# A planner's clock, its rule for early weights and its resting tiles, in an ordered two-block transformer kernel

## The chip, the cores and the metric

The kernel runs on one core of a Trainium2 chip. TensorE does the matrix products, ScalarE and VectorE the elementwise work, GpSimd a few small operations; transfers from device memory are issued from SyncE's queue. The metric is device time in microseconds (us) of one execution; lower is better.

## The reference

One sequence of 256 tokens, width 1024, float32 throughout, passes three layers. The first layer is a mixer (gated causal convolution and forgetting attention, one input projection) and a gated feed-forward of hidden width 2816. The second and third have attention (eight heads, a position bias; the third takes a difference of two softmaxes) and the same feed-forward, and each norm of them is modulated by a vector `c`:

```python
mod = (c_act @ ada_w[i] + ada_b[i])[:, None, :]
sh_a, sc_a, g_a, sh_f, sc_f, g_f = jnp.split(mod, 6, axis=-1)
h = rms_norm(x, norm_g[i, 0]) * (1.0 + sc_a) + sh_a
y = attention(h, ...)
x = x + g_a * rms_norm(y, norm_g[i, 1])
h = rms_norm(x, norm_g[i, 2]) * (1.0 + sc_f) + sh_f
x = x + g_f * rms_norm(swiglu_2(h, ffn_w_in[i], ffn_w_out[i]), norm_g[i, 3])
```

All weights are read once, some 227 MB in all, 50 MB of them `ada_w`.

## The kernel before

**Products.** Every large product is made of three products of fp32r operands. A weight tile of 128x512 float32 (called `raw` where the transfer puts it) is split into `hi` (ScalarE, a copy) and `lo` (VectorE, raw minus hi); activations are split the same way (`hTh`/`hTl`, `pair`). Three matmuls x_hi·w_hi, x_hi·w_lo, x_lo·w_hi add up in a bank of the matmul accumulator. The 256 tokens are two halves `h` of 128 rows. Split weights live in 16 pairs of slots (`hi`, `lo`), and in the feed-forwards in 8 more (`wp`). Transfers of `raw` go through three buffers of 1 MB.

**The order.** The program is one long order written by a planner that runs while the kernel is built. Class `Order` has a clock `now` that only TensorE's instructions and its idle time move: `mm` (a matmul) and `tr` (a transposition) add their planned time to it. Each other engine is a `Lane` with the time at which it comes free (`A` ScalarE, `V` VectorE, `G` GpSimd, `S` SyncE) and a cost for each operation. Tasks are generators that yield the time at which they go on; after each matmul `pump` runs the tasks whose time has come and then `fill`. So where an instruction stands in its engine's program depends on the planned times alone; on the chip every engine runs its own program strictly in that order and waits for what isn't ready. `pin` fixes the order.

**Weights.** `fill` issues the transfer of the next `raw` when a buffer is free by the plan, puts the next `hi` on ScalarE when the transfer has come by the plan (`come`) and ScalarE is free, and then `lo` on VectorE. `dma` plans a transfer at 360 bytes per ns after all transfers planned earlier, and 1.1 us more.

**Chains of norms.** `chain(h, ...)` is what stands between two big products: squares of the result (ScalarE), the root (`rstd`, GpSimd), the new `x` (VectorE, two instructions), its squares, the second root, the normalized tile `ch` (VectorE one half, ScalarE the other), eight transpositions on TensorE, modulation and splits. While half 0 is in its chain TensorE works on half 1's product. A chain raises `o.urgent`, and `fill` then takes weights only where an engine is free at once (slack 0 unless fewer than `ENOUGH` units are in stock). There are ten chains that end in transpositions and two, at the end, that end in the output.

**Modulation.** `ada` computes `c_act @ ada_w` on VectorE: 96 pieces of 512 KB go through two buffers `araw`, each with two multiply-adds into `asum`. Its pace follows the plan: piece i not before `t0 + i * ADA_EARLY`, never in a chain, and not while weights are short unless `t0 + i * ADA_LATE` has passed. Then `araws.give(t, r)` hands the buffer back at planned time r, and the next piece's transfer may be issued. All transfers of weights and of `ada_w` stand in one queue, SyncE's, in planned order; an issue that waits for its buffer holds back those behind it.

Of the kernel before, what the change touches and what calls it, by code (L numbers as in the profile page):

```python
# [13 lines left out]
F32R = mybir.dt.float32r  # L14
# [17 lines left out]
SLACK = 0.5  # L32
ENOUGH = 4
STOCK = 9
ADA_START, ADA_EARLY, ADA_LATE = 30.0, 5.5, 8.0
HEADS_1, HEADS_2 = 9.0, 2.0
PAD_END = 104
LAG = 3


# [67 lines left out]
class Order:  # L108
# [29 lines left out]
    def mm(self, out, lhsT, rhs, start, stop, shared=False):  # L138

        self.pin(self.pe, self.nc.tensor.matmul(out, lhsT, rhs, start=start, stop=stop, skip_group_check=shared))  # L140
        n = math.prod(out.shape[1:])
        self.now += n / 2400 * (1 if rhs.dtype == F32R else 4)
        return self.now + 0.2

    def tr(self, out, src, ident):
        self.pin(self.pe, self.nc.tensor.transpose(out, src, ident))  # L146
        self.now += 0.107
        return self.now + 0.2

    def spawn(self, gen, at=0.0):  # L150
# [62 lines left out]
def block_kernel(ctx: ExitStack, tc: tile.TileContext, a: dict, onehot: bass.AP, out: bass.AP):  # L213
    nc = tc.nc
    o = Order(tc)
# [7 lines left out]
    def ring(pool, name, n, shape, dtype=F32):  # L223
        return Ring([pool.tile(shape, dtype, name=f"{name}{i}") for i in range(n)])

    def small(name, shape, dtype=F32):
        return cst.tile(shape, dtype, name=name)
# [3 lines left out]
    araws = ring(cst, "araw", 2, [P, 1024])  # L231
# [32 lines left out]
    def ffn_stream(w_gu, w_dn, where):  # L264
# [3 lines left out]
        def up(s):  # L268
            for k0 in (0, 4):
                stream.append(Raw(gu[:, k0:k0 + 4, :, s * 256:(s + 1) * 256], 4, 512, where))  # L270

        def down(s):
            stream.append(Raw(dn[:, 2 * s:2 * s + 2, :], 2, 1024, where))
# [3 lines left out]
        for s in range(2, STEPS - 1):  # L277
            up(s)
            if s - 1 < STEPS - LAG:
                down(s - 1)  # L280
        up(STEPS - 1)
        for s in range(STEPS - LAG, STEPS):
            down(s)
# [21 lines left out]
    def issue_raw():  # L305
        r = stream[pos["raw"]]
        pos["raw"] += 1
        r.tile = raws.take()
        if len(r.ap.shape) == 4:
            dst = r.tile.rearrange("p (k g c) -> p k g c", g=2, c=r.w // 2)  # L310
            for g in range(2):
                r.arrival = o.dma(dst[:, :, g], r.ap[:, :, g])
        else:
            r.arrival = o.dma(r.tile[:, :r.nk * r.w].rearrange("p (k c) -> p k c", c=r.w), r.ap)

    def fill(force=False):

        slack = SLACK if not o.urgent or pos["lo"] - pos["first"] < ENOUGH else 0.0
        while True:
            while pos["raw"] < len(stream) and raws.when() is not None and raws.when() <= o.now:  # L320
                issue_raw()
            some = False
            if pos["unit"] < len(units) and pos["unit"] - pos["lo"] < 3:
                u = units[pos["unit"]]
                pool = more if u.where and more.when() is not None and more.when() <= o.now else slots
                come = u.raw.arrival is not None and u.raw.arrival <= o.now
                place = pool.when() is not None and pool.when() <= o.now
                if come and place and (force or A.free <= o.now + slack):
                    some = True
                    pos["unit"] += 1  # L330
                    u.pool, u.slot = pool, pool.take()
                    u.hi, u.lo = (t[:, :u.w] for t in u.slot)
                    u.hi_ready = A.activation(u.hi, u.raw.tile[:, u.at:u.at + u.w], AF.Copy)
            if pos["lo"] < pos["unit"]:
                u = units[pos["lo"]]
                if force or max(V.free, u.hi_ready) <= o.now + slack:
                    some = True
                    pos["lo"] += 1
                    u.ready = V.tensor_sub(u.lo, u.raw.tile[:, u.at:u.at + u.w], u.hi.bitcast(F32), after=u.hi_ready)
                    u.raw.left -= 1  # L340
                    if not u.raw.left:
                        raws.give(u.raw.tile, u.ready)
            force = False
            if not some:
                return
# [5 lines left out]
    def take(n):  # L351
        got = [u for r in stream[pos["use"]:pos["use"] + n] for u in r.units]
        pos["use"] += n
        return got
# [27 lines left out]
    def product(ps, pair, h, ks, us, marks=None, first=True, last=True):  # L382

        n = len(us)
        for i, (k, u) in enumerate(zip(ks, us)):
            if marks is not None:
                o.wait(marks[h][k // 4])
            c = slice(h * P, (h + 1) * P)
            t = triple(ps, pair[0][:, k, c], pair[1][:, k, c], u, first and i == 0, last and i == n - 1)
        return t  # L390
# [190 lines left out]
    def load_gain(src, gain):  # L581
        gain.tile = yield from o.get(gains)
        gain.load.t = o.dma(gain.tile, src.to_broadcast([P, D]))
# [46 lines left out]
    def ada():  # L630
        yield from o.until(c_mark)
        pieces = [(l, what, cc, k0) for l, what in ada_order for cc in range(2) for k0 in range(0, 8, 2)]
        loaded, t0 = [], o.now
        for i in range(len(pieces) + 1):
            if i < len(pieces):
                l, what, cc, k0 = pieces[i]
                c0 = parts_of.index(what) * D + cc * 512
                if k0 == 0:
                    if what[0] == "g" and cc == 0:
                        o.spawn(load_gain(a["norm_g_2"][l, 1 if what == "g_a" else 3].unsqueeze(0), gated[l, what]))  # L640
                    sums = yield from o.get(asum)
                    r = G.memset(sums, 0.0)
                    yield r
                    ba = o.dma(sums[0:1, :], a["ada_b_2"][l:l + 1, c0:c0 + 512])
                t = yield from o.get(araws)
                arrival = o.dma(t.rearrange("p (k c) -> p k c", c=512),
                                a["ada_w_2"][l].rearrange("(k p) c -> p k c", p=P)[:, k0:k0 + 2, c0:c0 + 512])
                loaded.append((l, what, cc, k0, t, max(arrival, ba), sums))
            if i:
                l, what, cc, k0, t, arrival, s = loaded.pop(0)  # L650
                yield max(arrival, t0 + i * ADA_EARLY)
                while (o.urgent or V.free > o.now + SLACK or
                       pos["lo"] - pos["first"] < STOCK and o.now < t0 + i * ADA_LATE):
                    yield o.now + 0.2
                for k in range(2):
                    r = V.scalar_tensor_tensor(s, t[:, k * 512:(k + 1) * 512], c_act[:, k0 + k:k0 + k + 1], s,
                                               op0=OP.mult, op1=OP.add)
                    yield r - 0.3
                araws.give(t, r)
                if k0 == 6:  # L660
                    o.spawn(ada_finish(l, what, cc, s, r), r)


    def scope(**kinds):

        stack, got = ExitStack(), {}
        for name, (n, shape, dtype) in kinds.items():
            got[name] = ring(stack.enter_context(tc.tile_pool(name=name, bufs=1, reuse_waits="tile")), name, n, shape, dtype)
        return stack, got
# [87 lines left out]

    small("pad_end", [P, PAD_END])
    phase, sc = scope(qp=(4, [P, 4, 256], F32), gp=(8, [P, 512], F32),
# [195 lines left out]
    for k0 in (0, 4):  # L955
        for h in range(2):
            t = product(fb[h][:, :260], hT, h, range(k0, k0 + 4), us_f[k0:k0 + 4], hm, k0 == 0, k0 == 4)
# [50 lines left out]
    for n in range(2):  # L1008
        us = take(1)
        o.wait(ya_mark)  # L1010
        for h in range(2):
            ps = o.hold(banks)
            t = product(ps, yaT, h, range(4), us)
# [22 lines left out]
    for h in range(2):  # L1036
        for n in range(2):
            ps = o.hold(banks)
            t = product(ps, ybT, h, range(4), ub[n])
# [23 lines left out]
    def ffn(hm, gb, **kw):  # L1063
# [25 lines left out]
        def up(s, h):  # L1089
            if s not in us_of:  # L1090
                us_of[s] = take(2)
            act_mark[s, h] = Mark()
            ps = o.hold(banks)
            t = product(ps, hT, h, allk, us_of[s], hm)
            o.spawn(activate(s, h, ps), t)
# [14 lines left out]
        def downs(s):  # L1110
            for h in range(2):
                for n in range(2):
                    down(s, h, n)
# [6 lines left out]
        for s in range(2, STEPS - 1):  # L1120
            up(s, 0)
            up(s, 1)
            if s - 1 < STEPS - LAG:
                downs(s - 1)
        us_of[STEPS - 1] = take(2)
        for s in range(STEPS - LAG, STEPS):
            dn[s] = take(1)
        for h in range(2):
            up(STEPS - 1, h)
            o.spawn(chain(h, ys[h], gb, out_marks, **kw))  # L1130
            for s in range(STEPS - LAG, STEPS):
                for n in range(2):
# [237 lines left out]
```

## Time and profile before

| | us |
|---|---|
| median of 3 runs | 990.28 (989.15 to 990.47) |
| the profiled execution, its own time | 993.5 |
| its span, first to last instruction | 991.6 |
| TensorE busy | 975.9 |
| VectorE busy | 739.2 |
| ScalarE busy | 605.2 |
| mean granted TensorE clock | 0.997 of full |

The rows come from the one profiled execution, whose time is 3.2 us above the median. A busy TensorE isn't proof of a full one: matmuls overlap in the records, so the rate is read from the starts of a run of them. In a timeline row the number in brackets is the idle time of the engine before the row and what ended it.

### The profile page before, as it was taken

How to read it: one execution, taken by the hardware profiler on the slowest of the kernel's cores; microseconds unless marked ns; L12 is line 12 of the kernel's file. 1: busy time of each engine (PE TensorE's matmuls, PEld its weight loads, DVE VectorE, ACT ScalarE, POOL GpSimd, SP SyncE). 2: the span in 40 equal slices, each digit the busy share in tenths (PEclk: the TensorE clock that was granted, in tenths of full speed). 3: DMA queues.
4: the chain of work that ended last, by engine and by line, in shares of the span. 5: the costliest groups of instructions: out<-in, count | busy, mean ns of one | idle time of the engine just before them, and what ended most of it. 6: DMA issues, size and time to landing. Idle time of an engine off the chain costs nothing.

```text
span 991.6 us, 14032 instructions
## 1 busy us (share of the span) xinstructions
PE 975.9 (98%) x4814; PEld 808.5 (82%) x4814; DVE 739.2 (75%) x1469; ACT 605.2 (61%) x1286; POOL 35.2 (4%) x65
## 2 busy tenths in 40 slices
PE   7999999999999999999999999999999999999997
PEld 6888778888888888898788888888897888888886
DVE  5897879889888958887799888747765786464632
ACT  6746666774555537866685454637788795464531
POOL 1000000000000001000000000001000100000000
PEclk9999999999999999999999999999999999999999
DMA  6969778679989875775759989645542567646401
GB/s 217 361 202 308 254 263 271 218 231 319 363 287 326 294 257 189 253 258 173 233 187 313 369 274 314 231 138 194 176 163 86 172 206 253 211 157 207 163 33 43
DMA packets 143539, 227.19 MB, mean 229 GB/s; under 512 B 5991, under 2 KB 78932, under 8 KB 143468
## 3 DMA queue, kind: packets, MB, share of 16 engines
q1 hardware_dynamic: 143452, 226.30, 68.0%
q8 instruction: 37, 0.61, 0.2%
q14 instruction: 34, 0.28, 0.1%
q10 hardware_dynamic: 16, 0.00, 0.0%
HBM read 225.22 MB, written 2.63 MB: 230 GB/s over the span
## 4 chain that ended last, share of the span: by engine, by line
PE 92%; DMA 3%; issue 2%; DVE 1%; ACT 1%; SPq 0%; POOL 0%; DVEq 0%; POOLq 0%; ACTq 0%
PE bank L140 87%; PE bank L146 5%; DMA raw<-in_w_in_dram 1%; DMA raw<-in_ffn_w_in_dram 1%; DMA araw<-in_ada_w_dram 1%; DVE lo L86 1%; DMA ep<-in_norm_g_dram 0%; SPq L134 0%; DVE asum L86 0%; ACT hi L86 0%; DVE x L86 0%; ACT junk L86 0%; POOL tiny L86 0%; DVE wp L86 0%; DVE ep L86 0%
## 5 line engine op out<-in xcount | busy, mean ns | idle before, releaser
L86 DVE TENSOR_TENSOR lo<-raw,hi 128x512 fp32r<-128x512 f32 (+1 forms) x499 | 322.8, 676 | 41.4 <-ACT hi L86 40.1
L86 ACT ACTIVATE hi<-raw 128x512 fp32r<-128x512 f32 (+1 forms) x499 | 298.0, 620 | 61.4 <-PE bank L140 33.1
L140 PE MATMUL bank<-hi,hTh 128*128 128x512 f32 (+1 forms) x672 | 263.6, 392 | 0.0
L140 PE MATMUL bank<-hi,hTl 128*128 128x512 f32 (+1 forms) x672 | 262.6, 391 | 0.0
L140 PE MATMUL bank<-lo,hTh 128*128 128x512 f32 (+1 forms) x672 | 262.2, 390 | 0.3 <-DVE lo L86 0.3
L140 PE MATMUL bank<-hi,pair 128*128 128x512 f32 x524 | 173.9, 396 | 0.0
L86 DVE SCALAR_TENSOR_TENSOR asum<-araw,c_act,asum 128x512 f32<-128x512 f32 x192 | 143.0, 745 | 7.5 <-DMA araw<-in_ada_w_dram 6.5
L140 PEld LDWEIGHTS bank<-hi,hTl 128*128 128x128 f32 x672 | 126.9, 189 | 25.5 <-issue 1.7
L140 PEld LDWEIGHTS bank<-lo,hTh 128*128 128x128 f32 x672 | 127.0, 189 | 24.0 <-DVE lo L86 0.6
L140 PEld LDWEIGHTS bank<-hi,hTh 128*128 128x128 f32 x672 | 127.1, 189 | 23.3 <-issue 0.2
L140 PE MATMUL bank<-wp,hTh 128*128 128x512 f32 x384 | 119.1, 391 | 0.0
L140 PEld LDWEIGHTS bank<-hi,pair 128*128 128x128 f32 x524 | 98.1, 189 | 19.5
L86 ACT ACTIVATE wp<-raw 128x512 fp32r<-128x512 f32 x145 | 88.5, 629 | 26.0 <-PE bank L140 16.7
L140 PE MATMUL bank<-lo,pair 128*128 128x512 f32 x262 | 103.9, 396 | 0.0
L86 ACT ACTIVATE ep<-bank 128x256 f32<-128x256 f32 x66 | 25.3, 383 | 125.8 <-PE bank L140 125.4
L86 DVE TENSOR_TENSOR wp<-raw,wp 128x512 fp32r<-128x512 f32 x145 | 94.9, 684 | 9.1 <-ACT wp L86 8.3
L140 PEld LDWEIGHTS bank<-wp,hTh 128*128 128x128 f32 x384 | 71.8, 188 | 15.0
L86 DVE TENSOR_TENSOR ep<-ep,bank 128x256 f32<-128x256 f32 x70 | 29.1, 416 | 70.8 <-ACT ep L86 70.2
L140 PE MATMUL bank<-wp,pair 128*128 128x512 f32 x294 | 76.7, 395 | 0.0
L140 PE MATMUL bank<-wp,hTl 128*128 128x512 f32 x192 | 75.1, 391 | 0.0
L140 PEld LDWEIGHTS bank<-wp,pair 128*128 128x128 f32 x294 | 54.3, 188 | 10.9
L86 ACT ACTIVATE pair<-bank 128x256 fp32r<-128x256 f32 (+1 forms) x74 | 28.8, 389 | 53.7 <-PE bank L146 42.4
(128 smaller groups left out, 952.4 us busy)
## 6 DMA issues: line engine op xcount, KB each, us to landing
araw<-in_ada_w_dram SPq DMA_DIRECT2D x96, 512.0 KB
raw<-in_ffn_w_in_dram SPq DMA_DIRECT2D x88, 512.0 KB
raw<-in_w_gate_up_dram SPq DMA_DIRECT2D x44, 512.0 KB
raw<-in_ffn_w_out_dram SPq DMA_DIRECT2D x22, 1024.0 KB
raw<-in_w_in_dram SPq DMA_DIRECT2D x18, 1024.0 KB
raw<-in_moba_w_qkv_dram SPq DMA_DIRECT2D x12, 1024.0 KB
raw<-in_diff_w_qkv_dram SPq DMA_DIRECT2D x12, 1024.0 KB
raw<-in_w_down_dram SPq DMA_DIRECT2D x11, 1024.0 KB
```

What stands on the lines that cost most here:

```text
L86: self.order.pin(self, fn(out, *args, **kw))
L140: self.pin(self.pe, self.nc.tensor.matmul(out, lhsT, rhs, start=start, stop=stop, skip_group_check=shared))
L146: self.pin(self.pe, self.nc.tensor.transpose(out, src, ident))
```

## The change

Three rules of the planner are changed; no instruction is added or left out, but all may be ordered otherwise.

1. The clock: a fp32r matmul counts 13.3 ns more than its columns at 2.4 GHz; a float32 one at least 218 ns; a transposition 98 instead of 107 ns. Four constants that are in planned us are made 5 to 7% larger (`ADA_EARLY`, `ADA_LATE`, `HEADS_1`, `HEADS_2`, the last two being the distance between the starts of attention heads).
2. In a chain, `fill` takes a weight tile only from 1.5 us after its planned landing (`LATE`).
3. A buffer of the modulation is free for its next transfer 3 us later than before (`SAFE`).

```diff
-ADA_START, ADA_EARLY, ADA_LATE = 30.0, 5.5, 8.0
-HEADS_1, HEADS_2 = 9.0, 2.0
+ADA_START, ADA_EARLY, ADA_LATE = 30.0, 5.8, 8.5
+HEADS_1, HEADS_2 = 9.6, 2.1
 PAD_END = 104
+PRODUCT = 0.0133
+LATE = 1.5
+SAFE = 3.0
...
-        self.now += n / 2400 * (1 if rhs.dtype == F32R else 4)
+        self.now += PRODUCT + n / 2400 if rhs.dtype == F32R else max(0.218, n / 600)
...
-        self.now += 0.107
+        self.now += 0.098
...
-                come = u.raw.arrival is not None and u.raw.arrival <= o.now
+                come = u.raw.arrival is not None and u.raw.arrival + (LATE if o.urgent else 0.0) <= o.now
...
-                araws.give(t, r)
+                araws.give(t, r + SAFE)
```

## Rows read from the trace of the kernel before

**Rows 1.** The page: busy us, share of the span and instructions of each engine.

```profile
PE 975.9 (98%) x4814; PEld 808.5 (82%) x4814; DVE 739.2 (75%) x1469; ACT 605.2 (61%) x1286; POOL 35.2 (4%) x65
```

**Rows 2.** Waits of TensorE: us in total, times, longest us; all six rows.

```profile
PE bank L146 <- DMA x<-in_x_dram: 5.8, 2, 4.1
PE bank L146 <- DVE ch L86: 2.2, 1, 2.2
PE bank L146 <- DMA ep<-in_norm_g_dram: 0.7, 1, 0.7
PE bank L146 <- DVE st L86: 0.3, 1, 0.3
PE bank L140 <- DVE lo L86: 0.3, 1, 0.3
PE bank L146 <- DVE ep L86: 0.2, 1, 0.2
```

**Rows 3.** Chain that ended last, in order of time: start us, us, what.

```profile
220.28 10.91 PE bank L140 x48
...
378.72 1.09 PE bank L146 x10
...
475.88 9.19 DMA raw<-in_ffn_w_in_dram
```

**Rows 4.** Timeline of VectorE, 482 to 488 us.

```profile
482.30 0.16 DVE L86 SCALAR_TENSOR_TENSOR tiny<-tiny 128x1 f32<-128x1 f32 x1 [0.89 <-ACT junk L86]
...
485.84 0.69 DVE L86 TENSOR_TENSOR lo<-raw,hi 128x512 fp32r<-128x512 f32 x1 [2.77 <-ACT hi L86]
486.45 1.41 DVE L86 SCALAR_TENSOR_TENSOR x<-ch,tiny,x 128x512 f32<-128x512 f32 x2
```

**Rows 5.** Timeline of GpSimd (the root) and of TensorE, same chain.

```profile
482.61 0.55 POOL L86 TENSOR_TENSOR tiny<-tiny,mhalf 128x1 f32<-128x1 f32 x1 [41.86 <-DVE tiny L86]
...
490.71 1.33 PE L146 MATMUL bank<-ident,ch 128*128 128x128 f32 x8 [2.20 <-DVE ch L86]
```

**Rows 6.** Windows 488 to 494.5 us: busy us by engine, granted clock, DMA share, GB/s.

```profile
488.00:490.70 2.70, 0.51 (x3) 0.09 (x1) 2.26 (x6) 2.30 (x6) 0.86 (x1) 1.00 0.05 20
491.50:494.50 3.00, 3.00 (x10) 2.42 (x9) 2.21 (x6) 1.34 (x4) 0.00 (x0) 0.50 0.96 325
```

**Rows 7.** Timelines of GpSimd, VectorE, ScalarE and TensorE, a chain elsewhere.

```profile
674.02 0.55 POOL L86 TENSOR_TENSOR tiny<-tiny,mhalf 128x1 f32<-128x1 f32 x1 [76.19 <-DVE tiny L86]
674.99 1.41 DVE L86 SCALAR_TENSOR_TENSOR x<-ch,tiny,x 128x512 f32<-128x512 f32 x2
672.99 0.60 ACT L86 ACTIVATE junk<-bank 128x512 bf16<-128x512 f32 x1 [0.73 <-PE bank L140]
679.98 1.04 PE L146 MATMUL bank<-ident,ch 128*128 128x128 f32 x8
```

**Rows 8.** Windows 474 to 486 us, the same columns.

```profile
474.00:478.00 4.00, 4.00 (x20) 3.30 (x19) 4.00 (x8) 2.29 (x5) 0.00 (x0) 1.00 0.75 235
478.00:482.00 4.00, 4.00 (x19) 3.31 (x18) 2.94 (x5) 1.25 (x4) 0.00 (x0) 1.00 0.82 248
```

**Rows 9.** Timelines of VectorE and TensorE, two chains with little room.

```profile
503.07 0.72 DVE L86 TENSOR_SCALAR ch<-x,tiny 128x512 f32<-128x512 f32 x1 [0.44 <-POOL tiny L86]
503.85 0.66 PE L146 MATMUL bank<-ident,ch 128*128 128x128 f32 x4
805.13 0.49 DVE L86 TENSOR_SCALAR ch<-x,tiny 128x512 f32<-128x512 f32 x1 [0.45 <-POOL tiny L86]
805.67 0.66 PE L146 MATMUL bank<-ident,ch 128*128 128x128 f32 x4
```

**Rows 10.** Waits of SyncE's queue, and the modulation's tile: first to last start.

```profile
SPq L134 <- DVE asum L86: 177.0, 74, 9.2
...
L86 DVE SCALAR_TENSOR_TENSOR asum<-araw,c_act,asum x192: 729/744/753, 41.3 to 628.5; 128x512 f32<-128x512 f32 x192
```

**Rows 11.** Timeline of VectorE, the chain behind the third layer's attention.

```profile
789.53 1.41 DVE L86 SCALAR_TENSOR_TENSOR x<-ch,tiny,x 128x512 f32<-128x512 f32 x2
```

## The prediction

> **What bounds the kernel now.** I read the page first: TensorE is busy 975.9 of the 991.6 us span, the next engine, VectorE, 739.2 [rows 1]. The waits of TensorE come second, since only they can be won: six rows with 9.5 us in all [rows 2]. The two that wait for the first input and for a norm's vector (5.8 + 0.7 us) are the start, before any rule of the change can act. What is left is 3.0 us, and 2.2 of it is one wait of a transposition (L146) for `ch`. The weights' splits hold TensorE up for 0.3 us, a feed-forward's `ep` for 0.2 us. So this planner is worth changing only in the chains of norms.
>
> The one long wait is followed back in the chain that ended last and in three timelines. It belongs to half 0 of the second layer's attention, whose chain runs under half 1's output product. VectorE's sum of squares stands at 482.30, the root is done on GpSimd at 482.61 + 0.55 = 483.16 us; `x` should follow at once, but starts only at 486.45 [rows 4, 5]. Between them in VectorE's order stands one `lo`, which began at 485.84 behind its `hi`, which waited for a transfer issued at 475.88 that took 9.19 us [rows 3, 4]. So `x` is 3.3 us behind the root. In a chain that isn't disturbed it is 674.99 - 674.57 = 0.4 us behind [rows 7]: the weight tile cost that chain 2.9 us, and TensorE waited 2.20 us for `ch` at 490.71 [rows 5]. It cost more: after 2.2 us with almost nothing to do (0.51 us busy in the 2.70 us from 488.0), the granted clock is 0.50, 1.2 GHz, in all of 491.5 to 494.5 us, and full before it [rows 6]. At half speed those 3 us do 1.5 us of work, so 1.5 us more are lost. The disturbed chain costs 2.2 + 1.5 = 3.7 us.
>
> **The change part by part.** *The clock.* A run of 48 products takes 10.91 us, 227.3 ns each [rows 3]. The old clock gives 512 columns / 2400 = 213.3 ns, 6.2% short; the new one 226.7, 0.3% short. Ten transpositions take 1.09 us, 109 ns each [rows 3]: old 107, new 98; a few hundred of them, so this is small. TensorE does the same instructions, so the direct cost is nothing; the effect is the order. Here is the part that speaks against it. The old clock's fault was a margin: whatever the plan gave ScalarE and VectorE to do under n products had 6% more time on the chip. From the second sum of squares to the transpositions a chain takes 679.98 - 672.99 = 7.0 us [rows 7]; 13.4 of 227.3 ns is 5.9%, and 5.9% of 7.0 us is 0.41 us by which the transpositions now come earlier in TensorE's order. Of the ten chains with transpositions, two have no room already: `ch` ends at 503.79 and 805.62, and the transpositions start 0.06 and 0.05 us later [rows 9]. These lose the whole 0.41 us; the disturbed chain is counted below, and the other seven have room for most of the loss. I take +0.8 us; nothing if rounding hides it, 10 x 0.41 = 4.1 us if every chain loses it.
>
> The 66 groups of feed-forward transpositions wait 0.2 us now [rows 2]. Their path is about 2 us (ScalarE 0.4, VectorE 0.4, three handovers), so they lose about 0.1 us each where there is no room. I take six such, +0.5 us (an estimate from those durations); the bounds are nothing and 66 x 0.1 = 6.6 us, near the lower end since only one of 66 waits at present.
>
> The Trainium skill, page "TensorE: Matmul & The Clock Gate", section "Back-to-back issue gap", gives a warm matmul its columns / 2.4 plus 2.5 ns, which is 215.8 ns here and would put the old clock right and the new one 5% slow. The row's 227.3 ns differs, so the row decides.
>
> *The four constants.* 5.8 / 5.5 = 1.055, 8.5 / 8.0 = 1.063, 9.6 / 9.0 = 1.067, 2.1 / 2.0 = 1.05, against the clock's 226.7 / 213.3 = 1.063. Measured in products they stay where they were, to 1%: nothing.
>
> *Later weights in chains.* `LATE` aims at exactly the disturbed chain. How late was that tile? The plan put `lo` ahead of `x`, so it saw the landing by 482.5 us at the latest (`hi` and `lo` in front of an `x` due at 483.6); it landed at 485.07. So the landing was at least 2.5 us behind the plan, more than 1.5. The plan moves transfers at 360 GB/s; the rows show 235 and 248 over 474 to 482 us [rows 8]. But 1.5 us are enough to put `lo` behind `x` by the plan, because `hi` is then taken from 482.5 + 1.5 = 484.0 and the root is there at 483.2. What can stay is a `hi` in front of the squares of `x` on ScalarE, which would be due at about 484.3 and have to wait for 485.7: 1.4 us of delay instead of 2.9. The chain then ends at 490.66 - 1.5 = 489.2 us or earlier, against TensorE's last product at 488.5. So TensorE waits 0 to 0.7 us there instead of 2.2, and with so short a wait I count no half clock: -3.7 + 0.3 = -3.4 us, between -3.7 and -1.5 (the wait is shortened and the clock falls all the same).
>
> The price is weights split 1.5 us later in each chain. What hides it is the stock of split slots: TensorE waits 0.3 us for `lo` in the whole execution [rows 2]. If that cover is gone at the head of a feed-forward, which takes 16 fresh units in its first 48 products, 1.5 us at each of six such places, 9 us; I take nothing.
>
> *Resting tiles.* SyncE's queue waits 177.0 us for `asum`, 74 times, up to 9.2 us each [rows 10], with weights' transfers behind it. A piece issued 3 us later by the plan finds its buffer free more often and lets weights through. TensorE doesn't wait for weights, so the gain is in landings alone, none counted. The price is a slower modulation: it ends at 629 us now [rows 10]; with two buffers a rest of 3 us costs at most 1.5 us per piece, and after the pause in the mixer some 70 pieces are left, so it ends by 629 + 105 = 734 us. All but its last eight pieces are wanted for the chain that has `x` at 789.53 [rows 11], the last eight at the end. Hidden; without that cover, TensorE would wait for what is left of the 105 us.
>
> **Sum.** -3.4 + 0.8 + 0.5 = -2.1 us, and the other waits for `st`, `lo` and `ep` (0.8 us, rows 2) are dealt anew: with transfers that land nearer their plan I take half of them away, -0.4. That is -2.5 us: 993.5 becomes 991.0 in the profiled execution's own time. The median is 3.2 us below that execution; I subtract the same from it, 990.28 - 2.5 = 987.8 us. What a measurement here can tell from no change is 0.2%, 2.0 us, so this lies just beyond it.
>
> **Rivals.** *The stall moves, or the median never had it* (no change). Every chain is ordered anew, and the plan's 360 GB/s is not touched; a landing 3 us late in another chain gives the 3.7 us back. It may also be that the median runs, 3.2 us shorter than the profiled one, lack most of the disturbed chain's 3.7 us already. Then the sum keeps only 0.8 + 0.5 - 0.4 = +0.9 us: 991.2; if half of the 3.7 us was there, 989.3. For it: the 3.2 us. Against it: the wait comes from the order and from rates that hold over 8 us.
>
> *The margin was what kept TensorE full* (slower). One mechanism: with the clock right, transpositions in all chains are due 0.41 us earlier, and a wait that is long enough brings the half clock. It decides from two chains whose wait reaches about 2 us, each at the 3.7 us of the one seen. With one removed and two made: 990.3 + 3.7 = 994.0 us. For it: the two chains with 0.05 us of room. Against it: `LATE` takes the weights out of the chains, and 0.41 us is far from 2.
>
> *The new clock runs slow* (no change). Were TensorE's products shorter than the new plan has them, by 5% say, every chain would be due another 0.35 us (5% of 7.0) early, at ten places 3.5 us: 987.8 + 3.5 = 991.3 us. For it no row speaks: the run of 48 products says 0.3%. The Trainium skill's formula above would make it so.
>
> *All waits go* (faster): -3.7 - 0.8 and no new ones, 985.8 us.
>
> **Chances and range.** Forecast 0.42, of which 0.38 lies below 988.3 (0.2% under the median) and 0.04 above it; all waits go 0.12; the stall moves or was absent 0.26; the new clock runs slow 0.01; margin 0.19. Faster 0.38 + 0.12 = 0.50; same 0.04 + 0.26 = 0.30 with the slow clock's 0.01 put to the slower side; slower 0.19 + 0.01 = 0.20. Predicted 987.8 us. The range reaches from 985.0, below the case where all waits go, to 992.6, which takes in the moved stall and the beginning of the margin case; about a tenth is left out at each end. The forecast's own range is 985.8 to 989.5 us.
>
> **What would show it.** Right: TensorE's row for `ch` falls below 1 us, the granted clock stays full through all ten chains, and in every chain `x` stands within 1 us of the root. Of the margin: rows of TensorE for `ch` and `ep` grow to about 1 us in sum. Of the resting tiles: SyncE's 177 us for `asum` shrinks, and the modulation ends between 629 and 734 us. The prediction is wrong if a window of granted clock 0.50 stands at another chain, or if `lo` holds TensorE for more than 1 us.

## The result and the profile after

The changed kernel takes 996.88 us (median of 9 runs, 994.05 to 1001.7) against 991.57 (989.15 to 992.87) on the same chips: ratio 1.0058, interval 1.0041 to 1.0075. It is slower by 0.6%; 987.8 was predicted, and the time lies above the range. The profiled execution is one of the slowest, 1001.26 us with a span of 999.5.

The page and the waits of TensorE after (us in total, times, longest) answer to [rows 1, 2]:

```profile
PE 979.9 (98%) x4814; PEld 808.6 (81%) x4814; DVE 742.8 (74%) x1469; ACT 606.8 (61%) x1286; POOL 40.6 (4%) x65
...
PE bank L149 <- POOL mk L767: 3.6, 1, 3.6
PE bank L149 <- DVE ep L89: 3.4, 4, 2.2
PE bank L149 <- DMA x<-in_x_dram: 2.5, 1, 2.5
PE bank L149 <- ACT ch L89: 2.4, 3, 2.0
PE bank L149 <- DMA ep<-in_norm_g_dram: 0.9, 1, 0.9
PE bank L143 <- DVE lo L89: 0.3, 1, 0.3
PE bank L149 <- DVE ch L89: 0.2, 1, 0.2
```

The start's waits (`mk`, `x`, the vector) have other names but 7.0 us against 6.5. What grew is `ep`, from 0.2 to 3.4 us, and `ch`, from 2.2 to 2.6, now in four waits instead of one. The windows of the two long ones, 499.4 to 501.5 and 640.0 to 642.5 us, and of what followed (columns as in [rows 6]):

```profile
499.40:501.50 2.10, 0.06 (x1) 0.00 (x0) 1.66 (x4) 1.13 (x3) 1.77 (x2) 1.00 0.32 88
502.60:505.80 3.20, 3.20 (x9) 2.46 (x9) 3.04 (x8) 3.17 (x8) 0.00 (x0) 0.50 0.62 253
640.00:642.50 2.50, 0.32 (x2) 0.00 (x0) 1.85 (x4) 0.37 (x1) 0.00 (x0) 0.99 0.65 249
642.60:645.80 3.20, 3.20 (x9) 2.62 (x10) 2.73 (x5) 1.54 (x3) 0.00 (x0) 0.50 0.60 175
```

After both waits the granted clock is 0.50 (1.2 GHz) for the whole window behind, as it was once before the change [rows 6]: each of the two costs 2.0 to 2.2 us and 1.6 us more at half speed.

The first stands in one of the two chains that had 0.05 us of room [rows 9]. From the start of its first root to the transpositions it takes 6.15 us (495.36 to 501.51), before 5.47 (498.38 to 503.85); its second root takes 1.47 us instead of 0.86. Without the wait the transpositions would come some 1.4 us earlier behind the first root than before, which is more than the clock's 6%; why was not followed.

The second is a new kind. Timelines of SyncE's queue, VectorE and TensorE, 631 to 643 us:

```profile
631.58 0.42 SPq L137 DMA_DIRECT2D araw<-in_ada_w_dram  x1
635.49 0.37 SPq L137 DMA_DIRECT2D raw<-in_ffn_w_out_dram  x1
635.95 0.53 SPq L137 DMA_DIRECT2D araw<-in_ada_w_dram  x1
...
640.61 1.54 DVE L89 SCALAR_TENSOR_TENSOR asum<-araw,c_act,asum 128x512 f32<-128x512 f32 x2 [5.14 <-DMA araw<-in_ada_w_dram]
642.07 0.41 DVE L89 TENSOR_TENSOR ep<-ep,bank 128x256 f32<-128x256 f32 x1
...
639.93 0.39 PE L143 MATMUL bank<-hi,hTl 128*128 128x512 f32 x1
642.53 0.69 PE L149 MATMUL bank<-ident,ep 128*128 128x128 f32 x2 [2.21 <-DVE ep L89]
```

VectorE stood still for 5.14 us in front of a multiply-add whose tile had not landed; the multiplication for a feed-forward (`ep`) stood behind it, and TensorE's two transpositions behind that. In the whole execution VectorE waits 33.5 us in 19 such places, against 6.5 in 7 before:

```profile
DVE asum L89 <- DMA araw<-in_ada_w_dram: 33.5, 19, 5.1
...
SPq L137 <- DVE lo L89: 530.1, 117, 17.7
...
SPq L137 <- DVE asum L89: 40.9, 21, 5.5
```

SyncE's waits for `asum` did shrink from 177.0 us to 40.9 [rows 10], while its waits for `lo` grew from 369.0 to 530.1.

**Waits counted by starts.** A busy record of a product lasts 0.39 us while products start every 0.227, so a wait shorter than some 0.2 us is hidden in the busy time and a longer one is shown too short (the row at 642.53 shows 2.21; its start is 642.53 - 639.93 = 2.60 us behind the last product's). For all comparisons below I therefore add up, from 150 us on, by how much a transposition starts later than 0.236 us after a product's start or 0.110 us after another transposition's, the usual distances, where that is over 0.06 us. Before: 4.0 us (`ch` 2.6, `ep` 1.2, the rest 0.2). After: 8.4 us (`ch` 3.4, `ep` 4.9, the rest 0.1).

### The profile page after: what moved, and what is told of

It is laid out like the page before. It is cut to its first block, busy times and chain, and to the rows that moved or that the text cites. A ratio compares the mean times of both kernels' runs of the same rounds, so it can differ in the third digit from the quotient of the medians.

```text
span 999.5 us, 13984 instructions
## 1 busy us (share of the span) xinstructions
PE 979.9 (98%) x4814; PEld 808.6 (81%) x4814; DVE 742.8 (74%) x1469; ACT 606.8 (61%) x1286; POOL 40.6 (4%) x65
## 4 chain that ended last, share of the span: by engine, by line
PE 83%; DMA 6%; DVE 5%; issue 2%; ACT 2%; POOL 1%; SPq 1%; DVEq 0%; POOLq 0%; ACTq 0%
PE bank L143 78%; PE bank L149 5%; DMA araw<-in_ada_w_dram 4%; DVE lo L89 2%; DMA raw<-in_w_in_dram 1%; POOL tiny L89 1%; DVE asum L89 1%; DMA raw<-in_ffn_w_in_dram 1%; DVE x L89 1%; DVE ch L89 1%; SPq L137 1%; ACT hi L89 0%; ACT junk L89 0%; DMA ep<-in_norm_g_dram 0%; DVE wp L89 0%
## 5 line engine op out<-in xcount | busy, mean ns | idle before, releaser
L143 PE MATMUL bank<-hi,hTh 128*128 128x512 f32 (+1 forms) x698 | 274.8, 394 | 0.0
L143 PE MATMUL bank<-lo,hTh 128*128 128x512 f32 (+1 forms) x698 | 274.1, 393 | 0.3 <-DVE lo L89 0.3
L143 PE MATMUL bank<-hi,hTl 128*128 128x512 f32 (+1 forms) x698 | 273.3, 392 | 0.0
L89 DVE SCALAR_TENSOR_TENSOR asum<-araw,c_act,asum 128x512 f32<-128x512 f32 x192 | 143.4, 747 | 35.1 <-DMA araw<-in_ada_w_dram 33.5
L143 PE MATMUL bank<-hi,pair 128*128 128x512 f32 x472 | 155.6, 393 | 0.0
L143 PE MATMUL bank<-wp,hTh 128*128 128x512 f32 x332 | 104.3, 395 | 0.1
L143 PEld LDWEIGHTS bank<-hi,pair 128*128 128x128 f32 x472 | 88.4, 188 | 17.9
L143 PE MATMUL bank<-wp,pair 128*128 128x512 f32 x372 | 93.8, 394 | 0.0
L143 PE MATMUL bank<-lo,pair 128*128 128x512 f32 x236 | 92.7, 393 | 0.0
L143 PEld LDWEIGHTS bank<-wp,pair 128*128 128x128 f32 x372 | 68.6, 188 | 13.8
L143 PE MATMUL bank<-wp,hTl 128*128 128x512 f32 x166 | 65.5, 395 | 0.0
```

What stands on the lines that cost most here:

```text
L89: self.order.pin(self, fn(out, *args, **kw))
```

## The experiments

Two theories at first. **Margin**: the old clock's fault of 6% was an allowance; with the true clock transpositions stand too early in TensorE's order, and it waits in front of them. **Resting**: a buffer that rests is refilled from behind weights' transfers and lands late, and VectorE stands still in front of what TensorE needs. Ratios are to the kernel before, run on the same chip, with 95% intervals; the waits by starts are those of the one profiled execution of each kernel.

| kernel | clock | LATE | SAFE | room | median us | ratio | waits by starts, us: all (`ch`, `ep`+`asum`) |
|---|---|---|---|---|---|---|---|
| before | old | 0 | 0 | 0 | 991.0 to 991.6 | 1 | 4.0 (2.6, 1.3) |
| changed | new | 1.5 | 3 | 0 | 996.88 | 1.0058 (1.0041 to 1.0075) | 8.4 (3.4, 4.9) |
| e1_no_rest | new | 1.5 | 0 | 0 | 1000.46 | 1.0090 (1.0077 to 1.0103) | 8.6 (0.3, 8.1) |
| e2_no_late | new | 0 | 3 | 0 | 995.84 | 1.0042 (1.0028 to 1.0057) | 5.8 (2.8, 3.0) |
| e4_clock_alone | new | 0 | 0 | 0 | 997.14 | 1.0056 (1.0044 to 1.0068) | 6.8 (2.3, 4.2) |
| e3_old_clock | old | 1.5 | 3 | 0 | 990.46 | 0.9990 (0.9980 to 0.9999) | 2.1 (1.3, 0.7) |
| e5_rest_alone | old | 0 | 3 | 0 | 989.48 | 0.9980 (0.9971 to 0.9989) | 1.0 (0, 0.6) |
| e6_late_alone | old | 1.5 | 0 | 0 | 989.87 | 0.9985 (0.9976 to 0.9994) | 1.1 (0.4, 0.6) |
| e7_room | new | 1.5 | 3 | all three | 991.68 | 1.0000 (0.9991 to 1.0010) | 1.1 (0.4, 0.8) |
| e9_room_chains | new | 1.5 | 3 | chains | 996.59 | 1.0051 (1.0037 to 1.0066) | 5.3 (2.0, 3.1) |
| e10_room_ffn | new | 1.5 | 3 | feed-forwards, modulation | 992.13 | 1.0006 (0.9997 to 1.0015) | 2.3 (1.3, 1.0) |
| e12_old_clock_room | old | 1.5 | 3 | all three | 990.22 | 0.9991 (0.9982 to 0.9999) | 1.0 (0.6, 0.1) |
| e8_slow_clock | 5.5% slow | 1.5 | 3 | 0 | 1009.19 | 1.0183 (1.0157 to 1.0210) | 18.2 (1.4, 15.0) |
| e11_fast_clock | 12% fast | 1.5 | 3 | 0 | 999.22 | 1.0079 (1.0066 to 1.0092) | 6.1 (1.6, 1.4) |

**Each part undone, and the clock alone.** The edits:

```diff
# e1_no_rest
-SAFE = 3.0
+SAFE = 0.0
# e2_no_late
-LATE = 1.5
+LATE = 0.0
# e3_old_clock: clock and the four constants as before the change
-        self.now += PRODUCT + n / 2400 if rhs.dtype == F32R else max(0.218, n / 600)
+        self.now += n / 2400 * (1 if rhs.dtype == F32R else 4)
-        self.now += 0.098
+        self.now += 0.107
# e4_clock_alone
-LATE = 1.5
-SAFE = 3.0
+LATE = 0.0
+SAFE = 0.0
```

> The changed kernel with the rest of the modulation's buffers set back to 0. Resting theory (a buffer that rests is refilled from behind weights' transfers in SyncE's queue, lands late, and VectorE stands still in front of what TensorE needs): VectorE's waits for araw fall from 33.5 us to about 7, the wait of 2.2 us for ep is gone, median about 991 to 992 us. Margin theory (the corrected clock makes transpositions due too early): nothing of that sort, about 996 us, waits of TensorE for ch and ep stay at some 6 us.

> The changed kernel with weights taken in chains as before (LATE 0). Resting and margin theory: not better than the changed kernel, about 996 to 999 us, with a weight tile in front of x in one chain or more. If the late weights themselves are the fault (weights that crowd behind the root): about 991 us, and GpSimd's root falls from 1.5 to 0.9 us.

> The changed kernel with the old clock and the old four constants, late weights and resting buffers kept. Margin theory: TensorE's waits for ch and ep fall from 6 us to below 2, no half clock, about 988 to 991 us. Resting theory: VectorE still waits some 30 us for araw, a wait of about 2 us for ep remains, about 994 to 996 us.

> The kernel before with the new clock and constants alone. Margin theory: slower than before by 3 us or more, about 995 us, with several waits of TensorE for ch and ep. Resting theory: within 2 us of before, 990 to 992 us.

The resting theory fell at once: without the rest the kernel is not faster but the slowest of the four, 1000.46 us, with VectorE's waits for `araw` down to 13.0 us. The margin theory's figure, about 996 us, is missed too; the waits for `ep` and `asum` are 8.1 us there. The old clock gives everything back, 990.46 us, and the clock alone costs 0.56%, as much as the whole change. Late weights are not at fault either (995.84 us without them). Of the e4 trace the first five rows of TensorE's waits:

```profile
PE bank L149 <- DMA x<-in_x_dram: 6.0, 2, 4.0
PE bank L149 <- DVE ch L89: 1.1, 3, 0.8
PE bank L149 <- DMA ep<-in_norm_g_dram: 1.1, 1, 1.1
PE bank L149 <- DVE asum L89: 0.9, 2, 0.7
PE bank L149 <- DVE ep L89: 0.9, 3, 0.4
```

There is no wait over 1 us behind the start, and the granted clock stays full until TensorE's last product, and still its span is 995.0 us. By starts there are twenty waits of 0.1 to 0.9 us, 6.8 us in sum. Against e6 below, the trace with the shortest span, e4 is 8.2 us longer, and 5.7 of them are these waits (1.1 us there); the other 2.5 us are spread over the products and weren't followed. So a long wait with the half clock is one form of the loss, not its cause.

**The rest and the late weights with the old clock.**

```diff
# e5_rest_alone: the kernel before, and
-                araws.give(t, r)
+                araws.give(t, r + SAFE)
# e6_late_alone: the kernel before, and
-                come = u.raw.arrival is not None and u.raw.arrival <= o.now
+                come = u.raw.arrival is not None and u.raw.arrival + (LATE if o.urgent else 0.0) <= o.now
```

> The kernel before with the resting buffers alone (SAFE 3, old clock, LATE 0). Margin theory: about 991 us, no slower than before, since the margin is there. Resting theory in its last form (the rest alone brings late landings of araw to VectorE): 994 us or more, VectorE's waits for araw over 20 us.

> The kernel before with late weights in chains alone (LATE 1.5, old clock, SAFE 0). If LATE is what takes the weight tile from in front of x at 490 us: no wait of 2 us and no half clock, 987 to 990 us. If the disturbed chain needs the rest too: about 991 us.

Both are faster than before, by 0.20% and 0.15%. In either trace the wait of 2.2 us at 490 us is gone and the granted clock stays full from the start's 15 us to TensorE's last product; e6's span is 986.8 us at a mean clock of 1.000. VectorE's waits for `araw` with the rest and the old clock:

```profile
DVE asum L89 <- DMA araw<-in_ada_w_dram: 5.3, 4, 3.0
```

So the 33.5 us of the changed kernel are not the work of the rest by itself: 5.3 us with the rest alone, 8.2 with the clock alone, 26.9 with both (e2). With the two together the multiply-adds stand in front of their landings; which of the plan's times is at fault was not taken apart.

**Room given back, and the clock pushed further.** If it is the margin, the true clock is harmless where the plan grants the room openly. Three places yield 0.4 us later before TensorE's transpositions are put into the order: behind `ch` in a chain, behind `ep` in a feed-forward, behind a modulation's sum.

```diff
# e7_room: all three; e9_room_chains: the second alone; e10_room_ffn: the first and third
+ROOM = 0.4
             r = V.tensor_mul(t, t, ps[:, 256:512])
             banks.give(ps, r)
-            yield r
+            yield r + ROOM
...
                 r = V.tensor_scalar(t, halves[n], rs[:, 0:1], None, op0=OP.mult)
-            yield r
+            yield r + ROOM
...
     def ada_finish(l, what, cc, sums, r):
-        yield r
+        yield r + ROOM
# e8_slow_clock
-ADA_START, ADA_EARLY, ADA_LATE = 30.0, 5.8, 8.5
-HEADS_1, HEADS_2 = 9.6, 2.1
-PRODUCT = 0.0133
+ADA_START, ADA_EARLY, ADA_LATE = 30.0, 6.1, 9.0
+HEADS_1, HEADS_2 = 10.2, 2.2
+PRODUCT = 0.0266
```

> The changed kernel, new clock and all, but TensorE's transpositions behind the feed-forwards' products, the chains and the modulation's sums are planned 0.4 us later. Margin theory: the many waits of 0.2 to 0.9 us in front of these transpositions go, 989 to 992 us. If the true clock harms in another way (another order of the queues, late landings): still about 996 us.

> The changed kernel with a clock that is 5.5% slower than TensorE (26.6 instead of 13.3 ns a product, constants stretched as much). Margin theory: the step from the old clock to the new one again, another 5 us or more, 1001 to 1006 us. If the true clock is only one order among many: 990 to 1000 us, no trend.

> The changed kernel with the 0.4 us of room in front of the chains' transpositions alone. If the chains are what the margin was for, as the prediction sized it: most of the gain of the room in all three places, 991 to 993 us. If the feed-forwards and the modulation are: 995 to 997 us.

> The changed kernel with the room in front of the feed-forwards' and the modulation's transpositions, none in the chains. If the chains are what the margin was for: 994 to 997 us. If the feed-forwards and the modulation are: 991 to 993.5 us.

The room gives back the whole loss (991.68, ratio 1.0000; e3, the same rules with the old clock, has 0.9990, and the intervals overlap). The clock moved on by the same step costs 12 us more, beyond the 1001 to 1006 us that the margin theory gave. Waits of TensorE, all of e7_room and the first rows of e8_slow_clock:

```profile
PE bank L150 <- DMA x<-in_x_dram: 6.2, 2, 3.8
PE bank L150 <- issue: 0.3, 1, 0.3
PE bank L144 <- DVE lo L90: 0.3, 1, 0.3
PE bank L150 <- DVE ep L90: 0.2, 1, 0.2
```

```profile
PE bank L149 <- DVE ep L89: 10.4, 13, 1.8
PE bank L149 <- DMA x<-in_x_dram: 6.4, 2, 4.0
```

In e7 the clock, the late weights and the rest are those of the changed kernel, and VectorE still waits 21.9 us for `araw`; what is gone is TensorE's waiting. Where the room is wanted, e9 and e10 tell: in the chains alone it gives 996.59 us, nothing that can be measured (1.0051 against 1.0058); in front of `ep` and the modulation's sums alone 992.13 us, all of it within the noise (1.0006 against 1.0000).

The traces show the lost room directly. For each of the 66 feed-forward groups I take the time from the end of VectorE's multiplication (`ep<-ep,bank`) to the start of the first transposition. Where that is under 0.15 us there is no room left, and TensorE has waited or was about to. There are 5 such groups before and 0 to 2 in the other orders with the old clock (e3, e5, e6, e12). There are 19 in the changed kernel, 13 to 21 in the others with the new clock and no room there (e1, e2, e4, e9), and 33 with the slow clock (e8). With the room there are 3 (e7) and 6 (e10).

**More margin than before.**

```diff
# e11_fast_clock
-ADA_START, ADA_EARLY, ADA_LATE = 30.0, 5.8, 8.5
-HEADS_1, HEADS_2 = 9.6, 2.1
-PRODUCT = 0.0133
+ADA_START, ADA_EARLY, ADA_LATE = 30.0, 5.2, 7.5
+HEADS_1, HEADS_2 = 8.4, 1.9
+PRODUCT = -0.0133
# e12_old_clock_room: e3_old_clock with the room in all three places
```

> The changed kernel with a clock 12% fast (minus 13.3 ns a product, constants shrunk as much), late weights and rest kept. Margin theory: waits of TensorE behind 200 us below 2 us in sum; the time stays within 2 us of the old clock's, 989 to 992 us, since there is hardly a wait left to win. If the trend goes on: 985 us.

> Old clock, late weights, rest and 0.4 us of room in all three places: the most margin short of a faster clock. Margin theory: the last waits of 0.3 to 0.8 us go, 987.5 to 990 us, the fastest of all. If more margin costs as much as it wins (banks and slots held longer): 990 to 992 us.

e12 is like e3 (990.22, 990.46): with the old clock the room has nothing left to win that can be measured, and the margin theory's figure (987.5 to 990 us, the fastest of all) is missed. e11 missed by far: 999.22 us instead of 989 to 992. Its waits for `ep` are small (1.4 us by starts, one of the 66 groups without room), but it waits 3.1 us for the queries' and keys' copies (`st`) and 1.6 for `ch`, and its products run 3 us longer in sum than before. A clock far too fast has a price of its own, which the margin theory doesn't hold; its cause wasn't followed.

## Why the prediction was wrong

- **The bound, the old stall and its price** were right. TensorE is still 98% busy, a wait of 2 us is followed by half clock each time (three times in the two profiles), and both `LATE` alone and the rest alone take the stall at 490 us away. In e6 `x` starts at 482.89, 0.03 us behind the root (482.31 + 0.55), as the prediction had it; with the clock alone a `lo` still stands between them, and `x` is 1.65 us behind (488.03 against 485.83 + 0.55). The rest wasn't aimed at that `lo`, so another order can move it too. Of the prediction's own signs of being wrong one came true: a window of granted clock 0.50 stands at another chain (502.6 us).
- **What that stall is worth to the median** was taken too high. The 3.7 us came from one profiled execution 3.2 us over the median; with the stall gone and the margin kept, the median falls by 0.15 to 0.20%, 1.5 to 2.0 us (e5, e6). The rival that the median lacked part of it fits that; no trace of a median execution shows it.
- **The step that failed** is the margin's price: "I take six such, +0.5 us" for the feed-forwards' transpositions. By starts, waits for `ep` and `asum` went from 1.3 to 4.9 us in the changed kernel, and to 4.2 with the clock alone; e10 shows that room in front of these two gives back 0.5%, some 5 us. No run tells the two apart in time, but all 4.9 us of the changed kernel are `ep`'s. Both factors were too small: 19 groups without room instead of six, and nine of them with waits of 0.1 to 2.4 us instead of 0.1 each. The reasoning behind the size was wrong too. It costed the path of one group, 2 us of work, of which 6% is 0.1 us. But `ep` isn't alone on its path: in VectorE's strict order it stands behind splits and multiply-adds, some of which wait themselves (the one at 640 us for its tile). In eight of the nine groups that wait by starts in the changed kernel, ScalarE's part was done 0.5 to 3.4 us before VectorE came to its own. One of them, in the timelines of ScalarE, VectorE and TensorE, with VectorE busy all the time:

```profile
521.83 0.38 ACT L89 ACTIVATE ep<-bank 128x256 f32<-128x256 f32 x1 [0.40 <-PE bank L143]
...
522.72 0.75 DVE L89 SCALAR_TENSOR_TENSOR asum<-araw,c_act,asum 128x512 f32<-128x512 f32 x1
523.38 0.69 DVE L89 TENSOR_TENSOR lo<-raw,hi 128x512 fp32r<-128x512 f32 x1
523.98 0.42 DVE L89 TENSOR_TENSOR ep<-ep,bank 128x256 f32<-128x256 f32 x1
...
524.45 0.44 PE L149 MATMUL bank<-ident,ep 128*128 128x128 f32 x2 [0.61 <-DVE ep L89]
```

The 6% was an allowance for that queue; 0.4 us at each place made up for it. The words "near the lower end since only one of 66 waits at present" took for idle room what was the margin at work, and it read the row of busy records: by starts five groups waited already, 1.0 us in sum. The upper bound written there, 6.6 us, was nearer to those 5 us than the value taken.

- **The chains** (+0.8 us) were right in sign and too small: 2.3 us of waits for `ch` with the clock alone, 0.9 of them in the chain that was disturbed before. Four of these five waits follow a second root of 1.5 us, a cost that the prediction didn't have (see below); e7 has four such roots and only 0.4 us of waits for `ch`. Room in the chains alone wins nothing back in time, so their weight in the median stays open.
- **Resting tiles**: "Hidden" holds with the old clock, where the rest even wins 0.2%. With the new clock VectorE's 33.5 us of waiting came with it. The modulation ended at 743 us, just beyond the 734 given as a bound.
- **The four constants** at nothing: not told apart from the clock by any run.
- **The rival "the margin was what kept TensorE full"** had sign and size (994.0 us) better than the forecast, but its place and its point of decision were wrong: it looked to the chains, where room alone wins nothing, and it asked for two waits of 2 us with the half clock. The profiled execution has exactly two, yet the clock alone loses as much with none.
- **The rival "the new clock runs slow"** finds no support: products start 0.227 us apart (median) in the changed kernel too.

What stays open: with the true clock and no room, orders that differ in `LATE` and `SAFE` lie 4.6 us apart (995.84 to 1000.46) with no part that explains it; and the changed kernel itself varies by 7.7 us from run to run, the kernel before by 3.7 in the same 9 runs. The missing allowance alone doesn't explain that: e1 and e4 lack it too and vary by 1.4 and 2.0 us in 5 runs.

None of these kernels adds the gain of the rest to that of the late weights (e3 has both and is at 990.46); the fastest is e5_rest_alone, 0.20% under the kernel before, and e6_late_alone isn't told apart from it.

## What to carry to other kernels

Where one engine is full and the others follow a fixed order, a cost model that errs fast for the full engine can be an allowance for everybody else (here 6% was; twice that, e11, cost 0.8%); before it is corrected, ask what the error paid for, and grant that openly in front of the full engine's dependent instructions (here 0.4 us in three places made up for 0.6%). Price a lost margin by the queue in front of the needed instruction, not by the instruction's own path. And count waits on a pipelined engine by starts: behind the start, e4's rows of waits come to 3.5 us, half of the 6.8 by starts.

## What the runs showed of the hardware

The root on GpSimd is one instruction on 128 elements in a chain of norms; there it takes 0.55, about 0.9 or about 1.5 us, by what VectorE does meanwhile. Timelines of GpSimd and VectorE, before (391.35) and after (391.70), the second root of the same chain:

```profile
391.35 0.87 POOL L86 TENSOR_TENSOR tiny<-tiny,mhalf 128x1 f32<-128x1 f32 x1 [3.31 <-DVE tiny L86]
391.13 0.68 DVE L86 TENSOR_TENSOR lo<-raw,hi 128x512 fp32r<-128x512 f32 x1
392.25 0.72 DVE L86 TENSOR_SCALAR ch<-x,tiny 128x512 f32<-128x512 f32 x1 [0.44 <-POOL tiny L86]
```

```profile
391.70 1.47 POOL L89 TENSOR_TENSOR tiny<-tiny,mhalf 128x1 f32<-128x1 f32 x1 [3.31 <-DVE tiny L89]
391.47 1.29 DVE L89 TENSOR_TENSOR lo<-raw,hi 128x512 fp32r<-128x512 f32 x2
393.20 0.72 DVE L89 TENSOR_SCALAR ch<-x,tiny 128x512 f32<-128x512 f32 x1 [0.44 <-POOL tiny L89]
```

With one `lo` beside it the root ends 0.41 us after that `lo` (392.22 against 391.81), with two back to back 0.41 us after the second (393.17 against 392.76): of the 0.55 us that it takes at its shortest, at most 0.14 are done beside them. Beside an operation that reads the accumulator's bank it takes 0.55 us (before, at 674.02, with `ch<-bank,gain` from 673.79 to 674.47). The Trainium skill, page "SBUF — State Buffer", section "SBUF: two separate sides", says that VectorE and GpSimd share a port pair as a lock held for a whole instruction, by a VectorE operation with two inputs in that memory too, and that the other blocks; the rows agree. No order with the old clock as it was (before, e3, e5, e6, e12) has a root of 1.5 us in its chains, and the orders with the new clock have three to seven. But e11, whose plan gives a product less time, has six: so it isn't shown why a second split comes to stand behind the sum. Where it does, the root takes 0.6 us longer (1.47 against 0.87).
